# Log-softmax over rows of 50,000: two stores and two loads in turns on one queue

## The chip, the cores and the metric

The kernel runs on one core of a Trainium2 chip. The metric is the device time of one execution in microseconds (us); the kernel before takes 7595.09 us, the median of 8 runs.

## The reference

The input is `x`, 16 x 512 x 50000 float32 numbers, 1638.4 MB; the output has the same shape. Each of the 8192 rows of 50,000 is turned into its log-softmax:

```python
max_x = np.max(x, axis=-1, keepdims=True)
shifted = x - max_x
log_sum_exp = np.log(np.sum(np.exp(shifted), axis=-1, keepdims=True))
return (shifted - log_sum_exp).astype(np.float32)
```

## The kernel before, in words

**Tiles.** A tile is 32 rows. Each row is cut into G = 4 parts of 12,500 elements, so a tile fills 128 partitions with 12,500 float32 each, 50,000 bytes a partition and 6.4 MB in all. There are 8192 / 32 = 256 tiles and NBUF = 4 buffers, `buf0` to `buf3`; tile t uses buffer t mod 4. The result is written over the input in the buffer, so a buffer goes through load, compute, store, and is then free for the next load.

**Compute.** VectorE takes a tile when its load has landed (`take(vector, landed[j])`). It finds the negated maximum of four pieces of 3,125 columns (`negm`, L206), and ScalarE follows piece by piece with the exponentials and their sums (`dump`, L242). VectorE then makes the maximum common to the four partitions of each row (L211, L174 to L189), ScalarE computes the factors that bring the four sums to that maximum (L250), VectorE multiplies (L217), TensorE adds over the four pieces and the four partitions (L270), ScalarE takes the logarithm (L236), and VectorE subtracts maximum and logarithm in the buffer (L194), which raises `subtracted[j]`. VectorE does the tiles strictly one after another; of the last tile, the subtraction and the store are cut into four pieces.

**Transfers.** All loads and stores are issued on SyncE's queue, by the program under `@block.sync`. `load(j, src)` (L144) starts the transfer of a tile into buffer j and lets it raise `landed[j]`. `store(j, dst, buf)` (L147) first waits for `subtracted[j]` and then starts the transfer out, which raises `stored[j]`. `take` (L43) waits on a semaphore and lowers it again. SyncE carries these out in program order, so a wait holds up whatever stands after it. A transfer raises its semaphore by 16, once for each of the 16 DMA engines, over which its 128 partitions are spread. A load of buffer j waits for `stored[j]`.

In the loop before, each of the 63 rounds has four turns. Turn j issues the store of the next buffer, k = j + 1, then waits until the store of buffer j has landed, and loads the next tile into j. The first store, of tile 0, stands ahead of the loop, and so the stores are one buffer ahead of the loads: S0 | S1 L0, S2 L1, S3 L2, S0 L3 | S1 L0, and so on. After the loop stand the stores of buffers 1, 2 and 3. `run(a, first, n)` makes the views of the input and the output that the rounds step through.

Of the kernel before, what the change touches and what calls it, by code (L numbers as in the profile page):

```python
# [17 lines left out]
R = P // G  # L18
C = 3125
NBUF = 4  # L20

NS = 4

# [19 lines left out]
def take(engine, sem, n=16):  # L43

    engine.wait_ge(sem, n).then_inc(sem, -n)  # L45


def cols(c):
    return slice(c * C, (c + 1) * C)
# [3 lines left out]
def kernel(  # L53
# [13 lines left out]

    rounds = (ntiles - NBUF) // NBUF
    assert ntiles % NBUF == 0 and rounds >= 2

    xt = xf.rearrange("(t r) (g w) -> t (r g) w", r=R, g=G)
    ot = of.rearrange("(t r) (g w) -> t (r g) w", r=R, g=G)

    def run(a, first, n):

        part = a[first : first + NBUF * n].rearrange("(q i) p w -> q i p w", i=NBUF)
        return lambda q, i: part[bass.ds(q, 1), i].rearrange("o p w -> (o p) w")
# [12 lines left out]
    ones = consts.tile([P, P], FP32, name="ones")  # L90
    bufs = [data.tile([P, W], FP32, name=f"buf{j}") for j in range(NBUF)]
    dump = dump_pool.tile([P, C], FP32, name="dump")
    sums = sum_pool.tile([P, NBUF], FP32, name="sums")
    rowsums = [sums[:, k : k + 1] for k in range(NBUF)]

# [15 lines left out]
    def sem(name):  # L111
        return ctx.enter_context(nc.semaphore(name))

    landed = [sem(f"landed{j}") for j in range(NBUF)]
    stored = [sem(f"stored{j}") for j in range(NBUF)]
# [13 lines left out]
    @block.gpsimd  # L129
    def _(gpsimd):  # L130
        view = ones.rearrange("p (r g) -> p r g", g=G)
        gpsimd.memset(ones, 1.0).then_inc(ready)  # L132
        gpsimd.affine_select(  # L133
            out=view, in_=view, pattern=[[-G, R], [0, G]], base=0,
            channel_multiplier=1, compare_op=ALU.is_ge, fill=0.0,
        ).wait_op(ready, 1, "sem-ge").then_inc(ready)
        gpsimd.affine_select(  # L137
            out=view, in_=view, pattern=[[G, R], [0, G]], base=G - 1,
            channel_multiplier=-1, compare_op=ALU.is_ge, fill=0.0,
        ).wait_op(ready, 2, "sem-ge").then_inc(ready)  # L140

    @block.sync
    def _(sync):
        def load(j, src):  # L144
            sync.dma_start(out=bufs[j], in_=src).then_inc(landed[j], 16)

        def store(j, dst, buf):  # L147
            take(sync, subtracted[j], 1)
            sync.dma_start(out=dst, in_=buf).then_inc(stored[j], 16)

        for t in range(NBUF):
            load(t, xt[t])
        store(0, ot[0], bufs[0])
        src, dst = run(xt, NBUF, rounds), run(ot, 1, rounds)
        with sync.Fori(0, rounds) as q:
            for j in range(NBUF):
                k = (j + 1) % NBUF
                store(k, dst(q, j), bufs[k])
                take(sync, stored[j])
                load(j, src(q, j))  # L160
        for j in range(1, NBUF - 1):
            store(j, ot[ntiles - NBUF + j], bufs[j])
        for c in range(NS):
            store(NBUF - 1, ot[ntiles - 1][:, cols(c)], bufs[NBUF - 1][:, cols(c)])
        for j in range(NBUF - 1):
            take(sync, stored[j])
        take(sync, stored[NBUF - 1], 16 * NS)
# [147 lines left out]
```

## Time and profile before

| | us |
|---|---|
| median of 8 runs | 7595.09 |
| lowest and highest | 7594.02, 7598.76 |
| the profiled execution | 7595.03 |
| its span in the profile | 7593.3 |
| busy: VectorE (DVE) | 5440.2 (72%) |
| busy: ScalarE (ACT) | 3184.8 (42%) |
| busy: TensorE matmuls (PE) | 477.8 (6%) |
| a load, from issue to landing (median of 256) | 44.2 |
| a store of a whole tile, likewise (median of 255) | 47.8 |

The profile describes one execution. Busy time of an engine says how long its instructions ran, not that anything waited for them; a row of the waits says who stood idle, until whose work ended, for how many us in total, how many times, and how long at most. `SPq` is SyncE's queue and `DVEq` VectorE's, and L45 is the line of `take`. The DMA rows give the share of time in which the 16 DMA engines moved packets, and the rate in GB/s. In a row of the stretches of time there stand the stretch and its length, then for PE, PEld, DVE, ACT and POOL the busy time with the number of instructions, then TensorE's granted clock, the DMA engines' busy share, and GB/s; the assignment of whole packets to a stretch by their start lets a share go slightly over 1 in a short one.

### The profile page before, as it was taken

How to read it: one execution, taken by the hardware profiler on the slowest of the kernel's cores; microseconds unless marked ns; L12 is line 12 of the kernel's file. 1: busy time of each engine (PE TensorE's matmuls, PEld its weight loads, DVE VectorE, ACT ScalarE, POOL GpSimd, SP SyncE). 2: the span in 40 equal slices, each digit the busy share in tenths (PEclk: the TensorE clock that was granted, in tenths of full speed). 3: DMA queues.
4: the chain of work that ended last, by engine and by line, in shares of the span. 5: the costliest groups of instructions: out<-in, count | busy, mean ns of one | idle time of the engine just before them, and what ended most of it. 6: DMA issues, size and time to landing. Idle time of an engine off the chain costs nothing. (4 is left out here: it accounts for less than half of the span.)

```text
span 7593.3 us, 14139 instructions
## 1 busy us (share of the span) xinstructions
PE 477.8 (6%) x2048; PEld 455.9 (6%) x2048; DVE 5440.2 (72%) x2819; ACT 3184.8 (42%) x2561; POOL 1.4 (0%) x7
## 2 busy tenths in 40 slices
PE   0000000000000000000000000000000000000000
PEld 0000000000000000000000000000000000000000
DVE  7777777777777777777777777777777777777776
ACT  4444443434444344443444434444344443434433
POOL 0000000000000000000000000000000000000000
DMA  9999999999999999999999999999999999999999
GB/s 425 430 432 433 432 432 434 433 432 433 434 433 432 433 434 432 432 433 434 432 432 434 434 432 432 434 433 432 433 434 433 432 433 434 433 432 432 434 434 390
DMA packets 74162, 3276.85 MB, mean 432 GB/s; under 512 B 8240, under 2 KB 8240, under 8 KB 8240
## 3 DMA queue, kind: packets, MB, share of 16 engines
q1 hardware_dynamic: 74160, 3276.83, 100.0%
q14 instruction: 2, 0.02, 0.0%
HBM read 1638.40 MB, written 1638.40 MB: 432 GB/s over the span
## 5 line engine op out<-in xcount | busy, mean ns | idle before, releaser
L242 ACT ACTIVATE dump<-buf,negm 128x3125 f32<-128x3125 f32 x1024 | 2937.2, 2868 | 3805.8 <-DVE negm L206 3708.4
L206 DVE TENSOR_REDUCE negm<-buf 128x1 f32<-128x3125 f32 x1024 | 3418.3, 3400 | 924.5 <-DVEq L45 924.5
L194 DVE TENSOR_SCALAR buf<-buf,negmax,logsum 128x12500 f32<-128x12500 f32 (+1 forms) x259 | 1738.8, 6714 | 553.9 <-ACT logsum L236 553.9
L270 PE MATMUL sums<-scaled,ones 128*128 128x1 f32 x2048 | 477.8, 355 | 7088.2 <-DVE scaled L217 7088.2
L270 PEld LDWEIGHTS sums<-scaled,ones 128*128 128x128 f32 x2048 | 455.9, 328 | 7110.0 <-DVE scaled L217 7110.0
L217 DVE TENSOR_TENSOR scaled<-scale,part 128x4 f32<-128x4 f32 x256 | 41.4, 162 | 580.4 <-ACT scale L250 580.4
L236 ACT ACTIVATE logsum<-sums 128x1 f32<-128x1 f32 x256 | 43.8, 171 | 551.0 <-PE sums L270 551.0
L242 ACT ACTIVATION_READ_ACCUMULATOR dump<-buf,negm 128x1 f32 x1024 | 190.9, 186 | 0.0
L250 ACT ACTIVATE scale<-negm,negmax 128x4 f32<-128x4 f32 x256 | 76.1, 297 | 23.6
L211 DVE TENSOR_REDUCE negp<-negm 128x1 f32<-128x4 f32 x256 | 40.1, 157 | 39.2 <-DVE negm L206 39.2
L189 DVE STREAM_TRANSPOSE negmax<-spread 128x32 f32<-128x32 f32 x256 | 54.2, 212 | 8.9
L174 DVE STREAM_TRANSPOSE allneg<-negp 128x32 f32<-128x32 f32 x256 | 54.1, 211 | 8.9
L177 DVE TENSOR_REDUCE rowneg<-allneg 128x8 f32<-128x32 f32 x256 | 47.6, 186 | 8.9
L183 DVE COPY spread<-rowneg 128x32 f32<-128x32 f32 x256 | 46.3, 181 | 8.9
L257 ACT ACT_TABLE_LOAD x1 | 1.3, 1283 | 1.0 <-SPq L109 1.0
L137 POOL TENSOR_SCALAR_AFFINE_SELECT ones<-ones 128x128 f32<-128x128 f32 x1 | 0.5, 518 | 0.1
L133 POOL TENSOR_SCALAR_AFFINE_SELECT ones<-ones 128x128 f32<-128x128 f32 x1 | 0.5, 517 | 0.1
L132 POOL MEMSET ones<- 128x128 f32 x1 | 0.2, 204 | 0.5 <-SPq L109 0.5
L299 POOL MEMSET const-bfloat16-1.0<- 128x1 bf16 x1 | 0.1, 101 | 0.0
L299 POOL MEMSET const-uint8-127<- 128x1 uint8 x1 | 0.1, 101 | 0.0
L299 POOL MEMSET const-float32-0.0<- 128x1 f32 x1 | 0.1, 98 | 0.3 <-issue 0.3
L299 POOL MEMSET const-float32-1.0<- 128x1 f32 x1 | 0.1, 98 | 0.0
## 6 DMA issues: line engine op xcount, KB each, us to landing
buf<-in_x_dram SPq DMA_DIRECT2D x256, 6250.0 KB, 44.2
out_dram<-buf SPq DMA_DIRECT2D x255, 6250.0 KB, 47.8
out_dram<-buf SPq DMA_DIRECT2D x4, 1562.5 KB, 11.7
```

Of the source, the lines that this page charges most:

```text
L174: vector.transpose(out=allneg, in_=negp.to_broadcast([P, SQ]))
L177: vector.tensor_reduce(out=rowneg, in_=allneg.rearrange("p (r g) -> p r g", g=G), op=ALU.min, axis=AX,)
L183: vector.tensor_copy(out=spread.rearrange("p (r g) -> p r g", g=G), in_=rowneg[:, :, None].to_broadcast([P, SQ // G, G]),)
L189: vector.transpose(out=negmaxs[k], in_=spread)
L194: ins = vector.tensor_scalar(out=buf, in0=buf, scalar1=negmaxs[k][:, 0:1], scalar2=logs[k], op0=ALU.add, op1=ALU.subtract,)
L206: vector.tensor_reduce(out=negms[j][:, c : c + 1], in_=bufs[j][:, cols(c)], op=ALU.max, axis=AX, negate=True,).then_inc(shifted.sem if c < ...
L211: vector.tensor_reduce(out=negp, in_=negms[j], op=ALU.min, axis=AX).then_inc(on_dve.sem)
L217: vector.tensor_mul(out=scaleds[j], in0=scales[j], in1=parts[j])
L236: scalar.activation(out=logs[k], in_=rowsums[k], func=ACT.Ln)
L242: scalar.activation(out=dump, in_=bufs[j][:, cols(c)], func=ACT.Exp, bias=negms[j][:, c : c + 1], scale=1.0, accum_out=parts[j][:, c : c + 1],
L250: scalar.activation(out=scales[j], in_=negms[j], func=ACT.Exp, bias=negmaxs[j][:, 0:1], scale=-1.0,)
L270: ins = tensor.matmul(rowsums[j], ones, scaleds[j][:, c : c + 1], start=c == 0, stop=c == NS - 1,)
```

## The change

The order of the stores and loads in the loop is changed. The loop's round has two halves of two buffers each (`PAIR = 2`). In each half the stores of both buffers are issued first, and then, for each of the two, the store is waited for and the next load is issued: S0 S1 L0 L1 | S2 S3 L2 L3. The store of tile 0 no longer stands ahead of the loop, so the destinations of a round begin at tile 0 in place of tile 1, and after the loop the stores of buffers 0 to 2 are issued instead of 1 and 2. Nothing else differs.

```diff
 C = 3125
 NBUF = 4
+PAIR = 2
...
         for t in range(NBUF):
             load(t, xt[t])
-        store(0, ot[0], bufs[0])
-        src, dst = run(xt, NBUF, rounds), run(ot, 1, rounds)
+        src, dst = run(xt, NBUF, rounds), run(ot, 0, rounds)
         with sync.Fori(0, rounds) as q:
-            for j in range(NBUF):
-                k = (j + 1) % NBUF
-                store(k, dst(q, j), bufs[k])
-                take(sync, stored[j])
-                load(j, src(q, j))
-        for j in range(1, NBUF - 1):
+            for pair in range(0, NBUF, PAIR):
+                some = range(pair, pair + PAIR)
+                for j in some:
+                    store(j, dst(q, j), bufs[j])
+                for j in some:
+                    take(sync, stored[j])
+                    load(j, src(q, j))
+        for j in range(NBUF - 1):
             store(j, ot[ntiles - NBUF + j], bufs[j])
         for c in range(NS):
             store(NBUF - 1, ot[ntiles - 1][:, cols(c)], bufs[NBUF - 1][:, cols(c)])
```

## The prediction

> **What bounds the kernel now.** The page's DMA rows come first, because every other engine has large idle shares.
>
> ```profile
> DVE  7777777777777777777777777777777777777776
> DMA  9999999999999999999999999999999999999999
> q1 hardware_dynamic: 74160, 3276.83, 100.0%
> HBM read 1638.40 MB, written 1638.40 MB: 432 GB/s over the span
> ```
>
> The 16 DMA engines are busy in every slice, all from one queue, SyncE's. DVE, the busiest compute engine, stands at 72%. Next, the waits: does compute ever hold the queue up?
>
> ```profile
> DVE negm L206 <- DVEq L45: 924.5, 249, 19.2
> SPq L45 <- SPq L45: 7303.5, 512, 41.8
> ```
>
> VectorE waits for a landed tile 249 times, 924.5 / 249 = 3.7 us each: compute is ahead of the transfers. SyncE spends its life in `take`. The stretches of time say how near to a ceiling the transfers are:
>
> ```profile
> 20.00:50.00 30.00, 1.87 (x8) 1.78 (x8) 25.28 (x13) 13.94 (x11) 0.00 (x0) 1.00 1.00 432
> 75.00:375.00 300.00, 20.53 (x88) 19.58 (x88) 229.22 (x120) 136.18 (x110) 0.00 (x0) 1.00 1.00 430
> 375.00:1075.00 700.00, 42.92 (x184) 40.95 (x184) 503.06 (x262) 297.65 (x237) 0.00 (x0) 1.00 1.00 433
> 4075.00:6075.00 2000.00, 125.03 (x536) 119.30 (x536) 1434.39 (x741) 838.89 (x673) 0.00 (x0) 1.00 1.00 433
> 7475.00:7593.30 118.30, 7.47 (x32) 7.13 (x32) 71.27 (x38) 37.49 (x32) 0.00 (x0) 1.00 0.85 365
> ```
>
> The last number of each row is GB/s. Only loads run from 20 to 50 us (the first store, issued at 45.25, stands behind them); later loads and stores alternate. The rate is the same, 433, apart from 430 in the first alternating 300 us and the tail. So alternating costs little once the kernel is under way. Last, SyncE's queue in mid-run, to see what stands in it:
>
> ```profile
> 3009.44 0.34 SPq L149 DMA_DIRECT2D out_dram<-buf  x1
> 3027.79 0.35 SPq L145 DMA_DIRECT2D buf<-in_x_dram  x1
> 3039.04 0.34 SPq L149 DMA_DIRECT2D out_dram<-buf  x1
> 3057.44 0.35 SPq L145 DMA_DIRECT2D buf<-in_x_dram  x1
> ```
>
> One turn takes 3057.44 - 3027.79 = 29.65 us, so a 6.4 MB transfer takes T = 14.8 us. The page's section 6 gives 44.2 us from a load's issue to its landing, that is 3 T: two transfers stand ahead of it. A tile's compute, from landing to store, is 26.2 us: VectorE starts the first tile at 19.17 and its store is issued at 45.25 (45.25 - 19.17 = 26.1); in mid-run from 3012.84 to 3039.04.
>
> **The change part by part.** Removed and added: nothing is. Still 256 loads, 259 stores, the same bytes, the same `take`s, and SyncE's instructions of 0.35 us are in other places. The order in the queue goes from S1 L0 S2 L1 S3 L2 S0 L3 to S0 S1 L0 L1 S2 S3 L2 L3. Four things can follow.
>
> *Does the queue run dry?* Before, a load is issued when its store has landed, with L(j-1) and S(j+1) queued: 2 T = 29.6 us of cover (44.2 - 14.8 = 29.4 from the page). After, when S0 lands only S1 is queued, and L0 is issued behind it; when S1 lands only L0 is queued, and L1 goes behind that. The cover is one T = 14.8 us. What must fit under it is the time to issue and start a transfer: the first load is issued at 1.04 and VectorE starts on it at 19.17, so 19.17 - 1.04 - 14.8 = 3.3 us, an upper bound because everything starts cold there. 3.3 is under 14.8, so the price is 0 for an engine that is not ahead of the others. Without the cover it would be up to 3.3 us for each of 252 loads, 830 us. The Trainium skill (DMA: Bandwidth & Descriptors, Anatomy of one DMA) speaks against the change here: a transfer pays a fixed cost of some 2.0 us, mostly the receipt of its last write, worst towards HBM, and the change waits on stores with less behind them. By that figure, 252 uncovered loads would cost 504 us; the row's cover says none is uncovered.
>
> *Does compute hold a store up?* Put L3's landing at 0; L2 landed at -14.8. DVE does tile 2 from -14.8 to 11.4, tile 3 from there to 37.3 (25.9 each back to back, 45.06 - 19.17 in the trace). The queue holds S0 S1 L0 L1 from 0 to 59.2, so S2 must be there by 59.2 and S3 by 74. SyncE comes to S2 only after it has issued L1, at 29.6, and S3 goes out at 37.3: 29 and 37 us early. What waits behind SyncE's wait for tile 3 is the `take` of S2, which lands at 74 anyway. At the start: S0 at 45.3, S1 at 71.3, the queue empty of neither (L3 lands near 65, S0 near 80), L1 near 94, S2 near 97, S3 near 123, while L0 and L1 fill the queue until 124. At the end L3 lands with S0 S1 S2 left before S3, 44.4 us, and tile 3 is done after 37.3: 7 us to spare, where before it was 7576.7 - 7573.6 = 3 us (L3 there at 7547, two stores of 14.8 behind it, and the last piece done after the 7.36 us of L194). Price 0.
>
> *The 16 engines do not march together.* The semaphore of a transfer is raised 16 times, once by each DMA engine, and the trace records each time. First to last they are 1.4 us apart at the first load, 3.7 us at 1.5 ms, 8.8 at 3.8 ms, 13.4 at 5.65 ms, 18.3 at the end: one engine falls back by 0.036 us a transfer. An engine ahead by more than 14.8 - 1.5 = 13.3 us (1.5 us: my estimate for the restart, under the 3.3) will find its ring empty in the new order. It then waits for the last one, which is never idle itself and alone sets the end (before, the others wait at the end instead: the tail's 365 GB/s). Price 0, at most the 18.3 - 13.3 = 5 us by which the leaders lose their lead.
>
> *Half as many turns from writing to reading.* The trace shows no direction change by itself, so it is bounded. Packets of 50,000 bytes take 1.847 us in the pure loads of the first 57 us and 1.850 to 1.852 on average in mid-run. The floor is 3276.83 MB at 433 GB/s = 7568 us, plus 3.3 at the start and 1.4 from the last landing to the end = 7573; the span is 7593, so 20 us is all that slow packets and turns together cost. Upper end of a gain: all of it, 20 us. Were all of it turns, half the turns would give 10 us. Lower end, a loss: S1 and S2 at the end of the kernel are the only two stores back to back, and their landings are 14.94 us apart against 14.88 for a store after a load (landing records). 0.06 x 128 pairs = 8 us. I take a gain of 3 us, mostly the 430 GB/s stretch at the start (300 x 3/433 = 2.1 us lost there, half of it back, and about as much in mid-run), as the pure and the mixed stretches differ so little.
>
> The sum against the profiled execution: 7593.3 - 3 = 7590 span; its own time was 7595.03, 1.7 more than the span, and the median of 8 runs is 7595.09, so nothing is lost in passing: 7590 + 1.7 = 7592 us. No change is what within 0.2% (15 us) means here; that is about what a measurement of this kernel tells apart.
>
> **The rivals.**
> *A, the forecast:* bandwidth is all, order is nothing. 7592, with 7585 (half the turns, 10 us) to 7603 (8 us lost) around it. For it: 433 GB/s in both the pure and the mixed stretch.
> *B, faster by over 0.2%:* turning is what makes the 20 us, and the pairs take nearly all of it away: 7595 - 18 = 7577. Against it: half the turns remain, and the engines, by then 4 to 18 us apart, write and read at the same time in any order.
> *C, slower:* the halved cover. Place: the issue of L0 and L2, after the first store of a pair. Point from which it decides: where the engine that is last is itself without a queued transfer, or where those that restart together delay it. If each pair from 5.6 ms on (lead over 13.3) pays the cold start of 3.3 us: (7593 - 5600) / 59.3 = 34 pairs x 3.3 = 112 us, 7707 us; with an eighth of that, 14 us, 7609. Against it: the last engine always has the whole next store ahead of it.
> *D, it does not do what it says:* the pairs stand in the queue, but the engines' spread mixes directions as before: 7595, inside A.
>
> The Trainium skill (DMA: Bandwidth & Descriptors, Where 436 GB/s comes from) puts the ceiling at 435.2 GB/s. By that 7529 us plus the ends would be the floor and B would have 60 us to find; no stretch of this trace sustains more than 433.
>
> **How the numbers follow.** A with D 0.85, B 0.05, C 0.10, of which a part ends within 0.2%. So faster 0.05, same 0.86, slower 0.09. The range, 7584 to 7609, is A's bounds with the 1 us of scatter below, and above reaches to the eighth of C.
>
> **What the profile would show.** Right: 432 GB/s, DMA nines throughout; a load's median landing falls from 44.2 to 29.6 us (T of cover and its own T), a store's is a mixture of about 44 (S0, S2: issued right behind a pair of loads, so 3 T) and 51 (S1, S3: landed at 88.8, issued at 37.3); VectorE's wait for loads keeps its 920 us but in about 125 pieces of 7 us (59.2 - 2 x 26.0). SyncE's stores come 7 to 26 us apart, its loads 14.8. The spread of the 16 engines stops at 13 to 14 us. Wrong: a DMA slice below nine in mid-run, GB/s below 430 there, or a turn of two tiles over 59.4 us, would show C; below 59.15 us, B.

## The result: 21 us slower, and the profile after

The changed kernel takes 7616.76 us (median of 12 runs) where the kernel before took 7595.69 (32 runs): a ratio of 1.0029, interval 1.0022 to 1.0037. No change had been forecast, 7592 us with a range up to 7609. The spans of the two profiled executions are 7614.2 and 7593.3 us, 20.9 apart.

The page of the changed kernel, rate by fortieths of the span, and its section of DMA issues:

```profile
GB/s 425 432 432 432 433 433 433 433 433 433 433 432 432 433 433 433 433 432 432 433 431 431 432 429 430 429 429 432 429 429 432 429 429 431 430 431 430 429 430 401
...
buf<-in_x_dram SPq DMA_DIRECT2D x256, 6250.0 KB, 29.4
out_dram<-buf SPq DMA_DIRECT2D x255, 6250.0 KB, 43.7
```

A load now lands 29.4 us after its issue: its own 14.8 and one transfer of cover, as the time is called that the transfers already queued give to the next one. The first half of the run has the rate of before; from the 21st slice on, about 3.8 ms, it is 429 to 432. Most of the loss comes late. The same in the stretches of time:

```profile
75.00:375.00 300.00, 20.53 (x88) 19.58 (x88) 230.44 (x121) 136.16 (x110) 0.00 (x0) 1.00 1.00 432
...
375.00:1075.00 700.00, 42.93 (x184) 40.96 (x184) 500.59 (x262) 298.20 (x239) 0.00 (x0) 1.00 1.00 433
...
4075.00:6075.00 2000.00, 125.08 (x536) 119.34 (x536) 1422.26 (x738) 833.17 (x670) 0.00 (x0) 1.00 1.00 430
6075.00:7475.00 1400.00, 87.73 (x376) 83.70 (x376) 998.28 (x518) 584.48 (x470) 0.00 (x0) 1.00 1.00 430
```

Compute is not what is late: VectorE waits for tiles as long as before, in half as many pieces of 953.1 / 125 = 7.6 us.

```profile
DVE negm L208 <- DVEq L46: 953.1, 125, 19.2
```

SyncE's timeline has the place. A row with "x2" merges two loads: each is issued the moment a store has landed, so its length less 0.35 us is the time from the landing of the first store of a pair to that of the second. The rows are from 3.05, 5.01 and 6.56 ms:

```profile
3047.07 15.27 SPq L146 DMA_DIRECT2D buf<-in_x_dram  x2
3062.59 7.18 SPq L150 DMA_DIRECT2D out_dram<-buf  x2
...
5008.41 15.43 SPq L146 DMA_DIRECT2D buf<-in_x_dram  x2
...
6556.33 15.32 SPq L146 DMA_DIRECT2D buf<-in_x_dram  x2
```

The second store takes 14.92 us at 3 ms and 15.08 and 14.97 later. From here on the text uses the landing records of the profiled execution, 16 for each transfer, one for each DMA engine. "Last engine" is the one whose records come last, "spread" the time from first to last, "lead" how far another engine is ahead of the last, "limit" the value at which the spread stops growing, "pace" the mean time between the last engine's landings, per transfer:

| stage | pace before | pace after | spread after, at its end | lost in the stage |
|---|---|---|---|---|
| 1 to 2 ms | 14.790 | 14.844 | 7.7 | 67 transfers x 0.054 = 3.6 |
| 2 to 4 ms | 14.818 | 14.838 | 11.7 | 135 x 0.020 = 2.7 |
| 4 to 7.44 ms | 14.818 | 14.884 | 11.8 | 231 x 0.066 = 15.2 |

The sum is 21.5 us; before 1 ms the two are equal to 0.2 us. The spread grows by 0.058 us a transfer between 1 and 2 ms, stops at 11.6 at 3.05 ms, and by 3.5 ms the middle engine's lead over the last one has stopped growing as well, at 11.1 us. After 4.3 ms the second store of a pair averages 15.1 us at the last engine instead of 14.91. The other three transfers of the turn are unchanged, or nearly: 14.91 for the first store, 14.76 and 14.77 for the loads.

### The profile page after: what moved, and what is told of

It is laid out like the page before. It is cut to its first block, busy times and chain, and to the rows that moved or that the text cites. A ratio compares the mean times of both kernels' runs of the same rounds, so it can differ in the third digit from the quotient of the medians.

```text
span 7614.2 us, 14202 instructions
## 1 busy us (share of the span) xinstructions
PE 477.9 (6%) x2048; PEld 455.9 (6%) x2048; DVE 5428.8 (71%) x2819; ACT 3184.8 (42%) x2561; POOL 1.4 (0%) x7
## 5 line engine op out<-in xcount | busy, mean ns | idle before, releaser
L208 DVE TENSOR_REDUCE negm<-buf 128x1 f32<-128x3125 f32 x1024 | 3417.3, 3399 | 953.1 <-DVEq L46 953.1
## 6 DMA issues: line engine op xcount, KB each, us to landing
buf<-in_x_dram SPq DMA_DIRECT2D x256, 6250.0 KB, 29.4
out_dram<-buf SPq DMA_DIRECT2D x4, 1562.5 KB, 11.7
```

Of the source, the lines that this page charges most:

```text
L208: vector.tensor_reduce(out=negms[j][:, c : c + 1], in_=bufs[j][:, cols(c)], op=ALU.max, axis=AX, negate=True,).then_inc(shifted.sem if c < ...
```

## The experiments

**Theory 1, the cover:** engines ahead find their rings (the lists of work of each engine) empty, bunch, and slow the last one. **Theory 2, pairing:** two transfers of one direction behind each other cost by themselves. Ratios are against the kernel before on the same chip, whose medians were 7593.5 to 7594.2 us.

### Does it repeat?

The changed kernel without an edit.

> The changed kernel once more, to see whether its trace repeats. Both theories expect about 7617 us. Theory 1 (cover: with one transfer of cover the engines ahead find their rings empty, bunch behind the last one, and their common turns slow it) expects the spread of the 16 engines to grow to 11 to 12 us by about 3 ms and to stop there, and the last engine's second store of a pair to go from 14.9 to 15.1 us after that. Theory 2 (pairing: two transfers of one direction behind each other cost more by themselves, whatever the cover) expects a turn of two tiles that is longer by the same 0.16 us (21 us over 128) from start to end.

It took 7611.46 us, 1.0024 (1.0010 to 1.0038). The spread stops at 11.6 us, at 3.2 ms; the second store goes from 14.9 to 15.1 after 4.3 ms. The loss per turn is not the same from start to end, where theory 2 expected that it is.

### Pairs early, pairs late

Pairs for 24 rounds, then the order of before (`pair_then_alt`); and the reverse after 42 rounds (`alt_then_pair`):

```diff
+        with sync.Fori(0, PAIRED) as q:      # 24 rounds of pairs
...
+        store(0, ot[done], bufs[0])
+        with sync.Fori(0, rest) as q:        # 39 rounds, one store and one load
```

> Pairs in the first 24 of the 63 rounds (to about 2.85 ms, before the spread was at its limit in the changed kernel), then the order of before. Theory 1: the part with the common turns never comes; what is left is the 0.02 to 0.05 us a transfer by which the last engine was slower in the changed kernel before 3 ms: 7595 to 7602 us, and the spread goes on past 12 us. Theory 2: 24/63 of 21 us, 8 us more than before, 7603 us.

> The order of before for 42 rounds (to about 5 ms, with a spread of about 12 us by then), one round of transition, then pairs for the last 20 rounds. Theory 1: the limit is there at once, and the pairs cost what they cost in the changed kernel after 4.5 ms, 0.06 us a transfer: 168 x 0.06 = 10 us, 7605 us. Theory 2: 21/63 of 21 us, 7602 us; the two differ in the trace, where theory 1 has the spread stop at 11.6 us and the second store of a pair at 15.1 us from the switch on, and theory 2 lets the spread go on.

Early pairs: 7600.48 us, 1.0024 (0.9999 to 1.0048; one of the four runs took 7646, the others 7599 to 7601), 6.9 us above before. Late pairs: 7602.62 us, 1.0012 (1.0002 to 1.0021), 9.1 us above. The totals are too near to both theories to decide. The records do; the execution profiled of the late pairs is the longest of its ten, 7607.87 us. With early pairs the last engine's pace goes from 14.84 back to 14.815 after the switch, and the spread goes on, to 22.5 us, at no cost. With late pairs it is 14.816 until the switch at 5 ms; then the spread is cut to 11.7 us, the second store takes 15.0 us in the first seven turns and 15.1 in the next, and the pace is 14.91 until 6 ms and later 14.87. The second load of a pair is slow there too, 14.9 us on average until 6 ms in place of 14.76. Stretches of the kernel with late pairs, ahead of and behind its switch:

```profile
4075.00:5000.00 925.00, 57.85 (x248) 55.20 (x248) 661.61 (x343) 385.50 (x310) 0.00 (x0) 1.00 1.00 433
5300.00:6000.00 700.00, 42.92 (x184) 40.95 (x184) 495.36 (x261) 295.29 (x237) 0.00 (x0) 1.00 1.00 429
```

So pairs below the limit cost 0.03 us a transfer against the same run's alternating part, and at the limit 0.055 to 0.095.

### Short cover without pairs

The order of before, with one more wait ahead of a load, on a signal `seen` from VectorE when a tile has landed (or from ScalarE after the tile's first piece), from round 8 on:

```diff
                 take(sync, stored[j])
+                take(sync, seen[(j - BACK) % NBUF], 1)
                 load(j, src(q, j))
...
             take(vector, landed[j])
+            vector.nop().then_inc(seen[j])
```

> The order of before, with a wait added ahead of each load for a signal that VectorE gives when it finds a tile landed; here it is the signal of the load before the last one, which has long been there. It only controls for the added instructions. Both theories: 7595 to 7597 us, the spread grows to about 18 us.

> The order of before (one store, one load in turns), but from round 8 on a load is also held back until the load before it has landed. Nothing is paired; the cover of a load goes from two transfers (29.6 us) to one (14.8 us). Theory 1: the spread stops at 11 to 12 us, from about 4.5 ms on, and from there the last engine loses some 0.2 us each tile: 3000/29.6 = 100 tiles x 0.1 to 0.2 = 10 to 20 us, 7605 to 7615. Theory 2: nothing is paired, 7595 to 7598 us.

> As the one before, but from round 8 on a load is held back until ScalarE has done the first piece of the tile loaded before it, some 6.5 us after its landing: the cover is about 14.8 - 6.5 = 8.3 us. Theory 1: the spread stops at about 8.3 - 3.2 = 5 us, from about 2.3 ms on, and the loss goes on for (7500 - 2300)/29.6 = 175 tiles x 0.1 to 0.2 = 18 to 35 us: 7613 to 7630. Theory 2: 7595 to 7600 us.

The control took 7596.42 us, 1.0004 (0.9994 to 1.0013). With one transfer of cover: 7601.88, 1.0011 (1.0001 to 1.0021), 5.5 us over the control. With 8.3 us of cover: 7605.51, 1.0017 (1.0007 to 1.0027). Both totals lie between what the two theories expected. The spread stopped where theory 1 said: 11.7 and 5.1 us. But the pace does not change when it does. With one transfer of cover the last engine's pace is 14.832 from 1.5 to 3 ms, ahead of the limit, and 14.831 to 14.835 behind it; with 8.3 us, where the limit is there from 1.1 ms on, it is 14.83 from 1.5 to 6.5 ms. The control has 14.82.

There is one exception. Two runs of ten with 8.3 us of cover took 7620 us, the profiled one among them, and it loses that time after 6.5 ms:

```profile
4075.00:6075.00 2000.00, 125.05 (x536) 119.31 (x536) 1432.40 (x739) 833.17 (x670) 0.00 (x0) 1.00 1.00 432
6075.00:7475.00 1400.00, 87.76 (x376) 83.73 (x376) 992.32 (x517) 584.43 (x470) 0.00 (x0) 1.00 1.00 427
```

From there its pace is 15.09, as the last engine's loads take 15.1 to 15.8 us in place of 14.75; its stores stay at 14.91. So an engine at the back can be slowed at the limit in alternating order too. What sets it off after 5 ms at the limit is not shown.

The stretches of the kernel with one transfer of cover show how to read the rate:

```profile
2075.00:4075.00 2000.00, 126.92 (x544) 121.10 (x544) 1431.61 (x746) 840.41 (x678) 0.00 (x0) 1.00 1.00 433
4075.00:6075.00 2000.00, 125.04 (x536) 119.30 (x536) 1432.57 (x740) 834.01 (x671) 0.00 (x0) 1.00 1.00 431
```

433 falls to 431 without a change of the last engine's pace, because 15 engines now keep to that pace: 6.4 MB / 14.832 us = 431.5 GB/s. The changed kernel's 430 is 6.4 / 14.884. So the limit by itself need not cost anything: apart from the exception it is free in alternating order, as the prediction said, and theory 1 in this plain form falls. Short cover costs a little, 0.012 us a transfer, long before the limit.

### Pairs with other covers

More cover, by cutting each transfer in two, so that half a load follows half a store. First by partitions:

```diff
+            for h in range(PARTS):
+                sync.dma_start(out=dst[half(h)], in_=bufs[j][half(h)]).then_inc(stored[h][j], 16)
```

> Pairs as in the changed kernel, but each load and store is two transfers of 64 partitions, and each half of a load is issued as soon as its half of the store has landed. The directions in the ring are the same; the cover goes from one transfer (14.8 us) to one and a half (22.2 us). It has 512 more semaphore packets for each DMA engine, 9 ns each, 4.6 us. Theory 1: the spread passes 12 us and the time is that of the alternating kernel in halves, within 6 us (7595 to 7606). Theory 2: 21 us above the alternating kernel in halves, 7617 to 7622.

> The control for the pairs in halves: the order of before (one store, one load), each in two halves of 64 partitions. Both theories expect the 4.6 us of the added semaphore packets and no more: 7595 to 7602 us, with a spread that grows to 17 or 18 us at the end.

These failed as experiments. Transfers of 64 partitions ran at little more than half the rate: 13438.96 us for the pairs (ratio 1.7694, 1.7646 to 1.7741), and in the control three runs of 13748 to 13836 and one of 7790, for which no interval can be given. From the page of the pairs in halves:

```profile
DMA packets 82339, 3276.89 MB, mean 243 GB/s; under 512 B 16416, under 2 KB 16416, under 8 KB 16416
```

Cut by columns, with all 128 partitions in each half:

> The order of before, each load and store as two transfers of all 128 partitions and half of the columns (packets of 25,000 bytes), a half of a load issued when its half of the store has landed. A control for the pairs in column halves. Twice the packets and semaphore packets: 5 to 30 us over before under both theories, spread growing to about 18 us.

> The changed order in column halves: directions in pairs as in the changed kernel, but the cover of a load is one and a half transfers (22.2 us) and not one (14.8 us). Theory 1 (short cover, then bunched leaders): the spread passes 12 us, the second store of a pair does not slow down to 15.1 us after 4 ms, and the time is within 8 us of the alternating kernel in column halves. Theory 2 (pairing by itself): 18 us above it.

The control took 7647.41 us, 1.0079 (1.0062 to 1.0096), one run of four at 7669; the pairs 7659.77, 1.0086 (1.0069 to 1.0103): 12.4 us apart, between 8 and 18. The spread of the control went on to 29 us, where 18 had been expected. The spread of the pairs went past 12, as expected, and then stopped at 19.2 us, at 3.95 ms: again some 3 us under the cover of 22.2. The pace of the pairs is 14.938 ahead of that and 14.945 to 14.961 after; the control's is 14.914 to 14.929. So most of the 12.4 us is a loss of 0.023 a transfer (512 x 0.023 = 11.8) that is there ahead of the limit, with one and a half transfers of cover just as with one (0.020 between 2 and 4 ms in the changed kernel). The pairs in columns, ahead of and behind the limit:

```profile
2075.00:3900.00 1825.00, 113.84 (x488) 108.61 (x488) 1293.50 (x671) 758.63 (x610) 0.00 (x0) 1.00 1.00 430
4075.00:6075.00 2000.00, 125.11 (x536) 119.37 (x536) 1421.29 (x738) 833.24 (x670) 0.00 (x0) 1.00 1.00 428
```

Less cover: the first load of each pair also waits until ScalarE has done one piece, or two, of the last landed tile.

```diff
                 for j in some:
                     take(sync, stored[j])
+                    if j == pair:
+                        take(sync, seen[(j - 1) % NBUF if held else (j + 1) % NBUF], 1)
                     load(j, src(j))
```

> The changed order; from round 8 on the first load of each pair is also held back until ScalarE has done the first piece of the last landed tile, some 3 us after its store has landed: cover about 11.6 instead of 14.8 us. Theory 1: the spread stops at about 8.5 us, from about 2.3 ms on, and the stretched turns (0.2 us for each pair) start there and not at 4 ms: (4000 - 2300)/59.4 x 0.2 = 6 us more than the changed kernel, about 24 us above before. Theory 2: as the changed kernel, 18 us above before.

> As the one before with the second piece: the first load of a pair about 6.5 us after its store, cover about 8.3 us. Theory 1: the spread stops at about 5 us, from about 1.4 ms on: (4000 - 1400)/59.4 x 0.2 = 9 us more than the changed kernel, about 27 us above before. Theory 2: 18 us above before.

7609.84 us, 1.0021 (1.0012 to 1.0031), and 7611.31, 1.0023 (1.0013 to 1.0033): 15.6 and 17.1 us above before, no more than the changed kernel's 18 in its repetition. The limits came out near those expected (8.5 and 5 us): 9.2 and 5.9 us, at 2.3 and 1.5 ms. The loss did not: theory 1 had 24 and 27 us. In the timeline the two loads stand closer, as the first is held back while the second still follows its store; from the kernel with two pieces:

```profile
2521.14 9.10 SPq L148 DMA_DIRECT2D buf<-in_x_dram  x2
2530.91 6.73 SPq L152 DMA_DIRECT2D out_dram<-buf  x2
```

The first load goes out 9.10 - 0.35 = 8.75 us ahead of the second store's landing. Here the second store averages 14.91 us after the limit, not 15.1, and the second load 14.78 to 14.98 by half milliseconds, not 14.77; the pace is 14.84 to 14.89 from 1 ms on.

### The transfers alone

No compute; 256 loads into two buffers and 256 stores out of two others, each issued when the transfer 2 or 4 places before it has landed. Data no longer tie the order to the cover.

```diff
+ORDER = [("S", 2), ("S", 3), ("L", 0), ("L", 1)]   # pairs; or S, L, S, L
+DEPTH = 2                                          # or 4
...
+            for i in range(4):
+                take(sync, done[i % DEPTH])
+                step(i, *moving(i, q))
```

> Transfers alone, no compute: the same 256 loads (into buffers 0 and 1) and 256 stores (of two tiles loaded once, from buffers 2 and 3), one store and one load in turns; each transfer is issued when the fourth before it has landed, so three transfers (44 us) of cover. Two loads ahead add some 33 us. Leaves out everything between load and store. Reference for the other three. Both theories: 14.80 to 14.82 us for a transfer of the last engine, about 7615 us.

> The same transfers alone, two stores and two loads in turns, the same three transfers of cover. Leaves out everything between load and store. Theory 1 (cover): as the alternating one, within 3 us. Theory 2 (pairing by itself): 0.022 us a transfer more, the excess seen in the pairs before the spread reaches its limit: 11 us above it.

> The same transfers alone, one store and one load in turns, each transfer issued when the second before it has landed: one transfer (14.8 us) of cover for every one. Leaves out everything between load and store. Theory 1: the spread stops at 11 to 12 us and the time is 5 us or more above the alternating one with deep cover. Theory 2: equal to it.

> The same transfers alone, two stores and two loads in turns, one transfer of cover. Leaves out everything between load and store. Theory 1: as the alternating one with one transfer of cover. Theory 2: as the pairs with deep cover. Both together: slowest of the four by 15 us or more, with the last engine's second store of a pair near 15.1 us once the spread has stopped at 11 to 12 us.

| | three transfers of cover | one |
|---|---|---|
| alternating | 7620.69 | 7620.68 |
| pairs | 7622.87 | 7621.87 |

Against the kernel before, the ratios are 1.0035 to 1.0039, with intervals from 1.0022 to 1.0053 (two more loads are in them). Pairs cost 1 to 2 us here, where theory 2 had 11, and the cover nothing. Theory 2 in its plain form falls as well. The paces are 14.801 and 14.805; the spread grows by 0.013 to 0.017 us a transfer, and that from 2 to 4 ms on only, to 9.0 at most, so no limit is reached and these runs say nothing of pairs at one. The rates of the pairs with one transfer of cover, from its page:

```profile
GB/s 419 430 432 432 432 433 433 432 433 433 433 433 433 433 433 433 433 433 432 433 433 433 433 433 433 433 433 433 433 433 433 433 433 433 433 433 433 433 433 413
```

### What in the compute drives the last engine back?

A third theory: the compute engines' traffic in SBUF. The changed order with most reads left out, and with most writes left out:

```diff
-                    out=negms[j][:, c : c + 1], in_=bufs[j][:, cols(c)],
+                    out=negms[j][:, c : c + 1], in_=bufs[j][:, few(c)],   # 64 columns for c > 0; ScalarE too
...
-[bufs[j]]
+[bufs[j][:, few(1)]]                                                   # the other kernel: 64 columns subtracted
```

> The changed order, in which VectorE's maximum and ScalarE's exponentials read 64 of 3125 columns in three of the four pieces; it leaves out the rest of them. Transfers, order, cover, and the subtraction in place are those of the changed kernel. Theory 3 (the compute engines' traffic in SBUF is what holds the last DMA engine back, and so drives the spread to its limit): if these reads are the cause, the spread grows by about 0.015 us a transfer as in the transfers alone and not by 0.056, it does not reach 11.6 us, and the time is near 7600 us. If not: spread at its limit from 3 ms, 17 us above before.

> The changed order, in which VectorE's subtraction in place does 64 of 12500 columns of a tile; it leaves out the rest (the last tile's is whole). Maximum and exponentials are whole. Theory 3 with the in-place writes as the cause: the spread grows by about 0.015 us a transfer, no limit, near 7600 us. If not: as the changed kernel, 17 us above before.

7610.67 us, 1.0022 (1.0012 to 1.0032), and 7624.36, 1.0039 (1.0024 to 1.0053). Theory 3 falls for each of the two alone: the spread still grows by 0.047 and 0.064 us a transfer and stops at 11.7. But the two are a test of the timing that was not planned. With few writes the spread stops at 2.5 ms and the middle engine's lead at 2.7, the second store reaches 15.1 us at about 3 ms instead of 4.3, and the kernel loses 30.6 us and not 18. With few reads they come at 3.4 and 3.6 ms, the second store rises only from 4.7 ms on, from 14.83 to at most 15.0, and the loss is 16.9 us. The kernel with few writes, in stretches:

```profile
1075.00:2075.00 1000.00, 63.47 (x272) 60.55 (x272) 491.98 (x367) 414.04 (x335) 0.00 (x0) 1.00 1.00 433
2075.00:4075.00 2000.00, 126.95 (x544) 121.13 (x544) 996.45 (x747) 843.67 (x680) 0.00 (x0) 1.00 1.00 431
```

No version of these is faster than the kernel before.

## Why the prediction was wrong, step by step

**Cover and compute (price 0): held.** The last engine never ran dry (its packets follow each other without a gap), and no store waited for compute: VectorE's wait is 953 us against 920 forecast, in 125 pieces. The loads' 29.4 us, the stores' issues 7 us apart, the nines of the DMA row and the gain in the first 300 us (430 to 432 GB/s, 1.4 us) came as written.

**The limit of the spread: right in kind, wrong in size.** 13.3 us from 5.6 ms on was forecast; it is 11.6 us from 3.05 ms on. The trace had offered 3.3 us for a restart, and the prediction took 1.5 instead, as its own estimate. Five kernels now give the restart as cover less limit: 14.8 - 11.6, 14.8 - 11.7, 22.2 - 19.2, 12.15 - 9.2 (from the loads' issue in the trace) and 8.75 - 5.9, that is 2.9 to 3.2 us. The Trainium skill (DMA: Bandwidth & Descriptors, Anatomy of one DMA) has a fixed cost of about 2.0 us, measured there on transfers issued from GpSimd; by this subtraction the whole way from a landing to the next packet is about 3 for these, issued from SyncE. No engine stands without a packet at the limit, though: the records show the time that the leaders give up as longer packets at the ends of transfers (2.01 us for the first engine's last packet of the second store between 4.5 and 6.5 ms, 1.85 between 2 and 3 ms). So "empty rings" is a reading. The other half of the miss is that the spread grew by 0.058 us a transfer, where the kernel before had shown 0.036: the prediction carried that rate over unasked.

**"Price 0, at most 5 us": the step that failed.** It reasoned that engines that wait cannot delay the one that never does. In alternating order that is so with one transfer of cover (14.832 us ahead of the limit and behind it), with the exception above at 8.3 us. In pairs it is not: 15.2 of the 21 us come after 4 ms, from the last engine's second store, 15.1 us for 14.91, and from a pace that was already 0.02 worse. In the packet records of 4.5 to 7.4 ms, packets that begin within 4 us after the first store's landing last 1.94 to 1.99 us on average, against 1.85 at the same place between 1.0 and 2.5 ms: there the bunched engines turn from storing to loading while the last one is at the beginning of its second store.

The last engine's own packets can be followed back from its landings, eight to a transfer. In its second store the second and third take 2.03 and 1.95 us between 4.5 and 5.5 ms, against 1.86 and 1.87 between 3.1 and 3.9 ms; the other six are as before. They run from about 1.4 to 5.3 us after the landing of the first store, and the other 15 engines end their second store 2.7 to 4.9 us after it, most of them before 3.8. Where the limit is smaller, so that the turn comes later in the last engine's transfer, the long packets come later too: the third and fourth at a limit of 9.2 us (1.88 and 1.89 us in the second load), the fifth at 5.9 (1.96), and the fifth to eighth in the exception above (1.96 to 2.21, limit 5.1). So the last engine is slowed at the place of the common turn.

That the turn is what slows it is a reading. For it also speaks that the stretch comes when the middle of the engines has come to the limit in three kernels (3.5, 3.6, 2.7 ms, the stretch some 0.3 to 1.1 ms later), and within a few turns where pairs are switched on at 5 ms, and that it is milder where the turn falls in another place (held loads, half columns).

**Rival C was the nearest, at a chance of 0.10.** The loss is at its place, and its condition, that those that restart together delay the last, is the reading above. The signs written for C came after 4 ms: 4 x 14.884 = 59.5 us for a turn of two tiles, and slices of 429 GB/s. Its price was not what was seen: 3.3 us for each pair of tiles were supposed, and 0.26 (4 x 0.066) measured, but from 4 ms on and not from 5.6, and 0.08 to 0.22 before.

**Order is nothing: held for transfers alone (1 to 2 us), not for this kernel.** Ahead of the limit the last engine falls back faster in pairs, by 0.020 to 0.023 us a transfer with one and with one and a half transfers of cover (and by 0.054 between 1 and 2 ms, where the kernel before had hardly begun to drift); 0.012 of such a loss appears with short cover and no pairs. Together some 6 us of the 21. Here the prediction had a gain of 3 us from fewer turns; only the 1.4 us of the first 300 us can be read as one. Its room of 20 us for turns rested on a rate shown to 1 GB/s, of which one is 17 us over the whole kernel, and the row of the pure loads shows 432, not 433.

**What stays open:** how the common turn slows the last engine, and why it does so in pairs and mostly not in alternating order; why one engine falls back at all, why it does so faster with compute beside it (0.036 to 0.058 us a transfer against 0.013 to 0.017), and why faster in pairs. Neither the reads nor the writes of the compute engines are the cause by themselves. A limit reached by the transfers alone was not tried.

## What to carry to other kernels

Here the DMA engines were full, the one of the 16 that was last set the end, and the rate in GB/s hid it: in such a kernel, read the first and the last of the 16 landings of a transfer and how the gap grows. An order of issue that lets loads wait on a store with only one transfer behind it bounded the engines' lead here to that transfer less about 3 us; this was free in alternating order and cost 0.07 us a transfer in pairs. A leftover that is "0 because it only delays engines that have time" deserves a row or a bound of its own, and where the trace has a duration for a restart, that goes into the sum.

## What the runs showed of the hardware that was not expected

Transfers of 64 of the 128 partitions, one half after the other, ran at 243 GB/s in pairs instead of 432, with packets of 50,000 bytes at 3.24 us on average instead of 1.85, though all 16 DMA engines were busy; in alternating order three runs of four were as slow, the profiled one at 237 GB/s, and one escaped it, at 7790 us. The Trainium skill (DMA: Bandwidth & Descriptors, Rules for kernel authors) advises against two transfers to disjoint halves because they serialize; that they can take 77% longer in all is this case's own number. Halving by columns cost 53 us in the alternating order (packets of 25,000 bytes at 0.932 us, where half of 1.852 is 0.926).
